# Sliding windows by DMA alone: 12 staged batches in place of 11, and nearly every direct DMA cut into 32 KB rows

## The chip, the cores and the metric

One core of one Trainium2 chip. The metric is the device time of one execution in microseconds. Executions of one kernel on one chip mostly agree within 0.3%. Every comparison of times below is made within one call (one session of runs), in which all kernels ran on the same chip beside runs of the kernel before. Each chip was used in one call only: what belongs to the chip and what to the call can't be told apart.

## The reference

The input `x` is 32 batches of 4096 rows of 256 floats. The output holds, for every batch, 127 windows of 64 rows, which start every 32 rows. Nothing is computed.

```python
n_windows = (length - window_size) // stride + 1      # 127
for i in range(n_windows):
    start = i * stride                                # stride 32
    result[:, i] = x[:, start:start + window_size]    # window_size 64
```

Think of a batch as 128 blocks of 32 KB (32 rows of 1 KB). Window `w` is block `w` followed by block `w + 1`, so nearly every block is written twice. The input is 134 MB, the output 266 MB.

## The kernel before

A batch goes one of two ways.

*Direct*: DMAs from DRAM to DRAM, issued from the sync queue. Every window is read and written: 8 MB through the DMA engines, 8 MB read and 8 MB written in HBM (the memory beside the chip, here the same as DRAM).

*Staged*: the 128 blocks are loaded once into a tile of 128 partitions (4 MB) and stored twice (8 MB), issued from the activation queue. The DMA engines carry 12 MB, HBM reads 4 and writes 8. A staged batch is therefore lighter on HBM and heavier on the DMA engines.

```python
DIRECT, IN, OUT = 32768, 16384, 16384    # packet sizes in bytes

def windows(self, q, b, w0, n, half=None):            # a direct DMA of n windows
    size = 2 * blk if half is None else blk           # half: only the first or second block of each
    off = blk if half else 0
    # out: n rows of `size` at window w0 of batch b; in: n rows, one block apart
    ...

class Staging:
    def run(self, q):                                 # groups of 6 batches: 6 loads, then 12 stores
        for first in range(0, len(self.batches), bufs):
            ...
            for g in group: self.load(q, g)
            for g in group: self.store(q, g)          # two stores of 128 rows of 32 KB each

# in the kernel:
staged = [*range(1, B - 3, 3), B - 2]                 # 11 batches; 21 are direct
for i, b in enumerate(direct):
    for j in range(7):                                # 7 times 16 windows, and later a "rest" of 15
        loading = turns < 102 or 306 <= turns < 391
        share += 5 if loading else 1
        cut = share >= 6
        turns += 4 if cut else 3
        if cut:                                       # two DMAs of 16 rows of 32 KB
            share -= 6
            c.windows(ring_d, b, w0 + 16 * j, 16, 0)
            c.windows(ring_d, b, w0 + 16 * j, 16, 1)
        else:                                         # one DMA of 16 rows of 64 KB
            c.windows(ring_d, b, w0 + 16 * j, 16)
    ...
```

The stores of a staged batch write 128 rows where 127 are wanted and so spoil one half window in each neighbouring batch. The "rest" DMA of the neighbour (15 windows) repairs it and waits for those stores. The last staged batch is stored exactly, in pieces of 112, 15, 15 and 112 rows.

`turns` is a count kept while the program is built. A DMA engine takes packets alternately from the two queues. A whole direct DMA gives each engine two 32 KB packets and one semaphore packet of 4 bytes (3 turns). A pair of cut ones gives two and two (4 turns). In as many turns the staged queue moves as many 16 KB packets. Cutting thus raises the staged share of the traffic.

## Time and profile before

| | before |
|---|---|
| time, median of the first 3 runs | 746.64 us (745.91 to 747.06) |
| time of the profiled run | 753.78 us (span 752.0) |
| direct 32 KB packets | 5334; shortest usual 1213 ns, mean 1239 |
| staged 16 KB packets | 8444; shortest usual 611 ns, mean 628 |
| semaphore packets | 4105; 9 ns |

The last three lines are from the packet records of the trace. "Shortest usual" is the value that more than half of the packets take; it is called the floor below.

These are lines of the page of the kernel before: the span, the busy share of the 16 DMA engines in 40 slices (tenths) and what they moved, the two queues (q1 direct, q10 staged; packets, MB, share of 16 engines' span) and the HBM traffic.

```profile
span 752.0 us, 308 instructions
...
DMA  9999999999999999999999999999999999999997
GB/s 372 422 419 432 424 435 427 414 426 416 416 425 422 423 424 416 422 421 420 421 421 395 424 423 424 431 429 417 429 416 414 416 422 425 417 429 420 417 393 302
DMA packets 17885, 313.16 MB, mean 416 GB/s; under 512 B 4105, under 2 KB 4105, under 8 KB 4105
...
q1 hardware_dynamic: 8881, 174.80, 55.2%
q10 hardware_dynamic: 9002, 138.35, 44.1%
...
HBM read 220.92 MB, written 266.99 MB: 649 GB/s over the span
```

The engines are busy up to the last slices, and the shares of the two queues add up to 99.3%. So an engine serves its packets one after another with hardly a gap, and the time is close to the sum of packet times on the engine that has the most. (The trace doesn't name the engine of a packet. How many packets an engine has is counted from the kernel; what is measured is the mean of all 16.)

The table of stretches of the same kernel (from and to in us, length, work of a compute engine, clock, DMA share, GB/s) shows the loads of a group of six (20 to 120, 420 to 510) and its stores (150 to 380, 535 to 660):

```profile
core 0: us, POOL busy (x), PEclk, DMA share, GB/s
20.00:120.00 100.00, 0.00 (x0) 1.00 1.00 424
150.00:380.00 230.00, 0.00 (x0) 1.00 1.01 422
420.00:510.00 90.00, 0.00 (x0) 1.00 1.00 425
535.00:660.00 125.00, 0.00 (x0) 1.00 1.01 419
```

The engines are full throughout, but in the store stretches they move 419 to 422 GB/s in place of 424 to 425. The packet records say why: direct packets take 1251 ns there, and 26% take more than 1270; in the load stretches they take 1219, and 2.5% do.

The DMA queues from 150 to 300 us (packets, MB, share), kernel before:

```profile
q1 hardware_dynamic: 1747, 36.18, 57.8%
q10 hardware_dynamic: 1745, 27.00, 42.7%
```

As many packets from one queue as from the other: this is the alternation by turns.

Two lines of the page's DMA issues (count, KB each, median us from issue to landing) show the mix of whole (1024 KB) and cut (512 KB) direct DMAs:

```profile
out_dram<-in_x_dram SPq DMA_DIRECT2D x92, 1024.0 KB, 100.3
...
out_dram<-in_x_dram SPq DMA_DIRECT2D x110, 512.0 KB, 91.0
```

### The profile page before, as it was taken

The page shows a single profiled execution, that of the slowest core. Times are in us where ns is not written, and L with a number is a line of the kernel's source. Part 1 is how long each engine was busy: PE and PEld are TensorE (multiplying, and loading weights), DVE is VectorE, ACT ScalarE, POOL GpSimd, SP SyncE. Part 2 cuts the span into 40 slices and gives each one's busy share as a digit, 9 for nine tenths or more (in the row PEclk, how much of TensorE's full clock was granted, in tenths as well). Part 3 has the DMA queues.
Part 4 walks back from the last instruction along what each step waited for, and adds up shares of the span by engine and source line. Part 5 has one row for each costly group of instructions (what it writes and reads, how often), then busy time and mean ns, then how long its engine had stood idle before and what let it go on. Part 6 is the DMA issues. An engine that isn't in the chain of part 4 may idle for free. (4 is left out here: it accounts for less than half of the span.)

```text
span 752.0 us, 308 instructions
## 1 busy us (share of the span) xinstructions
POOL 0.2 (0%) x4
## 2 busy tenths in 40 slices
POOL 0000000000000000000000000000000000000000
DMA  9999999999999999999999999999999999999997
GB/s 372 422 419 432 424 435 427 414 426 416 416 425 422 423 424 416 422 421 420 421 421 395 424 423 424 431 429 417 429 416 414 416 422 425 417 429 420 417 393 302
DMA packets 17885, 313.16 MB, mean 416 GB/s; under 512 B 4105, under 2 KB 4105, under 8 KB 4105
## 3 DMA queue, kind: packets, MB, share of 16 engines
q1 hardware_dynamic: 8881, 174.80, 55.2%
q10 hardware_dynamic: 9002, 138.35, 44.1%
q14 instruction: 2, 0.02, 0.0%
HBM read 220.92 MB, written 266.99 MB: 649 GB/s over the span
## 5 line engine op out<-in xcount | busy, mean ns | idle before, releaser
L187 POOL MEMSET const-bfloat16-1.0<- 128x1 bf16 x1 | 0.1, 103 | 0.0
L187 POOL MEMSET const-uint8-127<- 128x1 uint8 x1 | 0.1, 102 | 0.0
L187 POOL MEMSET const-float32-0.0<- 128x1 f32 x1 | 0.1, 100 | 0.2 <-issue 0.2
L187 POOL MEMSET const-float32-1.0<- 128x1 f32 x1 | 0.1, 99 | 0.0
## 6 DMA issues: line engine op xcount, KB each, us to landing
out_dram<-in_x_dram SPq DMA_DIRECT2D x92, 1024.0 KB, 100.3
out_dram<-xb ACTq DMA_DIRECT2D x20, 4096.0 KB, 142.4
out_dram<-in_x_dram SPq DMA_DIRECT2D x110, 512.0 KB, 91.0
xb<-in_x_dram ACTq DMA_DIRECT2D x11, 4096.0 KB, 124.0
out_dram<-in_x_dram SPq DMA_DIRECT2D x21, 960.0 KB, 99.2
out_dram<-xb ACTq DMA_DIRECT2D x2, 3584.0 KB, 100.5
out_dram<-xb ACTq DMA_DIRECT2D x2, 480.0 KB, 102.1
```

Source lines behind the costliest of these rows:

```text
L187: nc = _bacc.Bacc("TRN2", target_bir_lowering=False, num_devices=1)
```

## The change

The intent: give one more batch to staging, which takes traffic off HBM, and keep the two queues in balance by cutting nearly every direct DMA into 32 KB rows, in loads and in stores alike (12 of 12 and 11 of 12, in place of 5 of 6 and 1 of 6). The rests are issued when the count of turns says that the stores they wait for are done, with a slack of 34 turns.

```diff
-    staged = [*range(1, B - 3, 3), B - 2]
+    staged = [*range(1, B - 3, 3), B - 2, 0]
...
+    def rest_parts(b):
+        if len(waits[b]) == 2:            # batch 29 lies between two staged batches
+            return [(0, 8), (120, 7)]
+        return [(0 if b - 1 in spilled else 112, 15)]
...
-                loading = turns < 102 or 306 <= turns < 391
-                share += 5 if loading else 1
-                cut = share >= 6
-                turns += 4 if cut else 3
-                if cut:
-                    share -= 6
+                at = turns % (loads + per * stores)
+                share += 12 if at < loads else 11
+                if share >= 12:
+                    share -= 12
+                    turns += 4
...
+            rests.append(b)
+            rest(34)                      # rests whose stores are due, by the count of turns
```

More of the change, by code (lines that the diff above doesn't have):

```diff
@@ L33, in count, with windows @@
         self.total += 16
-    def windows(self, q, b, w0, n, half=None):
+    def windows(self, q, b, w0, n, half=None, piece=DIRECT, count=None):
         blk = self.blk
@@ L39, in windows @@
         off = blk if half else 0
-        self.count(
+        (count or self.count)(
             q.dma_start(
@@ L47, in windows @@
                 ),
-                max_dma_last_dim=DIRECT,
+                max_dma_last_dim=piece,
             )
@@ L132, with first @@
     spilled = staged[:-1]
-    def rest(b):
-        for n in (b - 1, b + 1):
-            if n in spilled:
-                st.wait_stored(ring_d, spilled.index(n))
-        c.windows(ring_d, b, 0 if b - 1 in spilled else 112, 15)
+    waits = {b: [g for g, n in enumerate(spilled) if abs(n - b) == 1] for b in direct}
+    per, loads, stores = 6, 6 * 17, 34
+    def first(b):
+        return 0 if b - 1 not in spilled else 8 if len(waits[b]) == 2 else 15
+    def rest_parts(b):
+        if len(waits[b]) == 2:
+            return [(0, 8), (120, 7)]
+        return [(0 if b - 1 in spilled else 112, 15)]
@@ L141, with stored_turn @@
+    def stored_turn(b):
+        return max(
+            [(g // per) * (loads + per * stores) + loads + (g % per + 1) * stores for g in waits[b]],
+            default=0,
+        )
     with tc.tile_critical():
         st.run(ring_s)
-        free = [b for b in direct if b - 1 not in spilled and b + 1 not in spilled]
-        direct = free + [b for b in direct if b not in free]
-        late = 8
-        share = turns = 0
-        for i, b in enumerate(direct):
-            w0 = 15 if b - 1 in spilled else 0
-            for j in range(7):
-                loading = turns < 102 or 306 <= turns < 391
-                share += 5 if loading else 1
-                cut = share >= 6
-                turns += 4 if cut else 3
-                if cut:
-                    share -= 6
-                    c.windows(ring_d, b, w0 + 16 * j, 16, 0)
-                    c.windows(ring_d, b, w0 + 16 * j, 16, 1)
-                else:
-                    c.windows(ring_d, b, w0 + 16 * j, 16)
-            turns += 3 if b in free or i >= len(free) + late else 0
-            if b in free:
-                rest(b)
-            elif i >= len(free) + late:
-                rest(direct[i - late])
@@ L168, with rest @@
-        for b in direct[-late:]:
-            rest(b)
+        turns = share = 0
+        rests = []
+        def rest(slack):
+            nonlocal turns
+            for b in list(rests):
+                if turns >= stored_turn(b) + slack:
+                    rests.remove(b)
+                    for g in waits[b]:
+                        st.wait_stored(ring_d, g)
+                    for w, n in rest_parts(b):
+                        c.windows(ring_d, b, w, n)
+                        turns += 3
@@ new lines @@
+        for b in direct:
+            for j in range(7):
+                at = turns % (loads + per * stores)
[3 more added lines that the diff above has]
+                    turns += 4
+                    c.windows(ring_d, b, first(b) + 16 * j, 16, 0)
+                    c.windows(ring_d, b, first(b) + 16 * j, 16, 1)
+                else:
+                    turns += 3
+                    c.windows(ring_d, b, first(b) + 16 * j, 16)
+            rests.append(b)
+            rest(34)
@@ L170 @@
+        rest(-10000)
         ring_d.wait_ge(c.done, c.total)
```

## The prediction

> **What bounds the kernel now.** The 16 DMA engines, which are full. The page's slices show DMA 9 up to the second last; the stretches table a DMA share of 1.00 with 419 to 425 GB/s from 20 to 675 us. The queue lines give 55.2% (direct) and 44.1% (staged) of 16 engines' span: packets are served one after another without gaps. By the trace's packet records a direct 32 KB packet takes 1213 ns at its floor, mean 1239; a staged 16 KB packet (load or store) 611, mean 628; a 4-byte semaphore packet 9. An engine moves 27 GB/s whatever the kind, so a staged batch (4 MB in, 8 MB out) costs it more than a direct one (8 MB). Its only gain is less HBM traffic (now 649 GB/s).
>
> That gain shows in the excess over the floors. In load stretches (20-135, 430-525 us), where most direct DMAs are already cut into 32 KB rows, direct packets take 1220 ns and 3% exceed 1270. In store stretches (160-395, 545-675 us), where one in six is cut, they take 1250 to 1255, and 26 to 28% exceed 1270: the mix is somewhat over what HBM serves.
>
> **The change.** The Trainium skill, "DMA: Bandwidth & Descriptors", section "Queues, rings and completion order", says that an engine alternates between queue rows packet by packet. The trace agrees: 1747 and 1745 packets from 150 to 300 us. A semaphore packet takes a turn, so cutting lets the staged queue move more bytes per direct byte. Turns per engine: 559 direct, 561 staged before; 615 and 612 after: balanced.
>
> - Removed per engine (0 to 6): 14 direct packets of 336, -17.0 us. The average engine loses 15.9: batch 29's rest becomes 8 + 7 windows, and by the same page's section "Why a DMA increments its semaphore by 16 and not by 1" a DMA of 15 rows uses 15 engines (3547 semaphore packets = 202x16 + 21x15 confirm it), so 8 and 7 rows load engines 0 to 6 twice.
> - Added: 48 staged packets, +29.3 us; about 73 semaphore packets, +0.7.
> - Floor of the fullest engine: 732.5 -> 745.5 us, +13.0.
> - Recovered: the stores' excess. I estimate direct packets at 1221 ns (as in load stretches), loads 625, stores 618: 393 + 120 + 237 + 3 = 753 us, against 416 + 332 + 2 = 750 now.
>
> All of it is on the critical path. Waits for stored tiles (64 us in two on the direct queue's issuer) cost nothing now, since issues run about 100 us ahead; the slack of 34 turns (estimate 45 us) should keep the queue full.
>
> So better HBM service and added bytes nearly cancel: +3 us on 746.6; zero excess would give -5. **Predicted 749 us, 743 to 757; faster by over 2%: 0.02; within: 0.94; slower: 0.04.**
>
> **What would show it.** Right: 317.4 MB in place of 313.2; HBM read about 216.8 MB; direct packets at 1215-1225 ns in store stretches, few over 1270; 424 to 430 GB/s there; both queues end together. Wrong: direct packets at 1240 or more in stores (then +10 us); a hole in the direct queue at a rest's wait; one queue outlasting the other.
>
> **What would make it wrong.** Excess set by HBM writes, not total traffic; more DMAs (293 for 223) making the issuer late; engines 0 to 6 ending over 2 us after the others.

The stretches named in it were read on the packet records' own clock, which runs 11 us ahead of the page's. The numbers of this document are read on the page's clock; they differ from those by less than 5 ns.

## The result, and the profile after

Ratios in this document are the mean time of one kernel's fast runs over that of the other's of the same rounds, so not quite the ratio of the medians that stand beside them.

| | before | after |
|---|---|---|
| time, median | 746.5 us (745.91 to 747.06, 4 runs) | 754.42 us (753.03 to 755.05, 4 runs) |
| ratio | | 1.0104 (95%: 1.0086 to 1.0121) |
| direct 32 KB packets, mean | 5334 at 1239 ns | 5080 at 1217 ns |
| staged 16 KB packets, mean | 8444 at 628 ns | 9212 at 617 ns |
| all packet times, per engine (mean of 16) | 747.1 us | 744.6 us |

The packets of before are those of its profiled run of 753.78 us, not of a run of 746.5. Profiles of both kernels on one chip stand under "Both kernels again".

The same lines of the page, kernel after:

```profile
span 752.5 us, 382 instructions
...
DMA  9999999999999999999999999999999999999995
GB/s 376 432 432 432 432 431 420 432 432 431 432 432 430 442 422 431 443 429 423 415 429 423 432 438 424 431 435 431 432 427 431 431 429 437 427 430 417 412 388 218
DMA packets 19552, 317.43 MB, mean 422 GB/s; under 512 B 5258, under 2 KB 5258, under 8 KB 5258
...
q1 hardware_dynamic: 9732, 166.48, 51.7%
q10 hardware_dynamic: 9818, 150.93, 47.3%
...
HBM read 216.79 MB, written 267.06 MB: 643 GB/s over the span
```

There are 4.3 MB more for the engines and 4.1 MB less to read from HBM, as intended. The rate of most slices rises to 430 GB/s and over. The last slice falls to 218 in place of 302: the engines are busy for 5 tenths of it in place of 7.

The same stretches, kernel after:

```profile
20.00:120.00 100.00, 0.00 (x0) 1.00 1.01 431
150.00:380.00 230.00, 0.00 (x0) 1.00 1.00 429
420.00:510.00 90.00, 0.00 (x0) 1.00 1.00 429
535.00:660.00 125.00, 0.00 (x0) 1.00 1.01 432
```

Stores now run as fast as loads, 429 to 432 GB/s. In the store stretches the direct packets take 1217 ns (1.3% over 1270) and the staged ones 612: the excess is all but gone. Sixteen engines at the floor of 32768 bytes in 1213 ns would move 432 GB/s, so this kernel stands at the limit of its engines.

The queues from 150 to 300 us, kernel after: they still alternate, but with more bytes on the staged side.

```profile
q1 hardware_dynamic: 1985, 33.59, 52.2%
q10 hardware_dynamic: 1998, 30.90, 48.1%
```

The same two kinds on the page of the kernel after:

```profile
out_dram<-in_x_dram SPq DMA_DIRECT2D x265, 512.0 KB
...
out_dram<-in_x_dram SPq DMA_DIRECT2D x8, 1024.0 KB
```

So the profile after shows nearly every packet faster than the profile before, and yet the kernel is 1% slower. The experiments are about this.

### The profile page after: what moved, and what is told of

Its sections match the earlier page's. It is cut to its first block, busy times and chain, and to the rows that moved or that the text cites. A ratio compares the mean times of both kernels' runs of the same rounds, so it can differ in the third digit from the quotient of the medians.

```text
span 752.5 us, 382 instructions
## 1 busy us (share of the span) xinstructions
POOL 0.2 (0%) x4
## 2 busy tenths in 40 slices
DMA packets 19552, 317.43 MB, mean 422 GB/s; under 512 B 5258, under 2 KB 5258, under 8 KB 5258
## 3 DMA queue, kind: packets, MB, share of 16 engines
q1 hardware_dynamic: 9732, 166.48, 51.7%
q10 hardware_dynamic: 9818, 150.93, 47.3%
HBM read 216.79 MB, written 267.06 MB: 643 GB/s over the span
```

## The experiments

Three calls were made. All twelve runs finished; the result of one is wrong, on purpose. The chips of the three calls are called B, A and C, by what they did with the kernel before: B and C took 753.5 and 753.9 us for it, A took 747.1.

| run | chip | time, us | ratio to before (95%) | direct, staged packet, ns |
|---|---|---|---|---|
| before again | B | 752.96 | 0.9985 (0.9965 to 1.0005) | 1237, 627 |
| before, third | C | 753.77 | 0.9997 (0.9984 to 1.0009) | 1238, 627 |
| after again | B | 756.76 | 1.0038 (1.0020 to 1.0056) | 1220, 619 |
| after, third | A | 754.23 | 1.0109 (1.0085 to 1.0133) | 1216, 617 |
| after, fourth | C | 757.33 | 1.0042 (1.0029 to 1.0055) | 1219, 619 |
| 11 staged, all cut | B | 758.70 | 1.0065 (1.0046 to 1.0084) | 1254, 619 |
| 12 staged, old cuts | B | 774.91 | 1.0272 (1.0243 to 1.0300) | 1239, 640 |
| 12 staged, whole rows, same mix | A | 754.11 | 1.0098 (1.0081 to 1.0114) | 1218, 617 |
| 11 staged, even cuts | A | 745.37 | 0.9984 (0.9966 to 1.0002) | 1225, 623 |
| 11 staged, even cuts, again | C | 753.97 | 0.9995 (0.9983 to 1.0007) | 1235, 631 |
| 12 staged, batch 29's rest spread | A | 751.12 | 1.0061 (1.0044 to 1.0078) | 1216, 617 |
| 12 staged, last store whole (wrong result) | C | 756.20 | 1.0031 (1.0018 to 1.0044) | 1220, 617 |

The theory: the time is the sum of packet times on the fullest engine. The change adds 13.0 us to that sum at the floor and takes away the excess over the floor, which stems from more HBM traffic than HBM serves. How much excess there is to take away depends on the chip. The rivals: the form of the rows (64 or 32 KB) and not the mix of traffic sets the excess; the many small DMAs cost the 8 us; the end of the kernel does.

### Both kernels again, on three chips

No edit. The kernel before:

> The kernel before, unchanged, profiled again. Theory A: the profiled execution of before (753.8 us) was a poor sample of its timed runs (746.5), so its excess over the floors was overstated: a run near 746 should show direct packets at about 1228 ns and staged ones at about 621, sum of packet times about 740 us per engine in place of 747. Rival: the profiler itself costs this kernel 7 us every time: again about 753 us when profiled, direct 1239, staged 628. Ratio 1.000 in either case.

> The kernel before, unchanged, for a profile on whichever chip this call gets. Theory (its excess depends on the chip): if this call's times are near 747, direct packets at about 1227 ns and staged about 622, sum of packet times about 741 us per engine; if near 753, 1237 and 627, as in the earlier look, sum 746. Rival (the difference between chips lies outside the packets, in start or end): 1237 and 627 in either case.

The kernel after:

> The changed kernel, unchanged. Both theories: about 754 us, ratio 1.010; direct packets 1217 ns, staged 617, sum of packet times 745 us per engine.

> The changed kernel again, as the reference for the other runs of this call. Before moved between two chips (746.5 and 753.5 us) and the changed kernel less (754.4 and 756.8). Theory: before runs at the edge of what HBM serves and so shows the chip's state, the changed kernel runs at the engines' floor and does not: 754 to 757 us, ratio 1.003 to 1.011, high where before is near 746. Rival: the chips differ alike for both kernels: a ratio that stays at the same value whatever before shows.

> The changed kernel as reference of this call: 754 to 757 us; direct 1216 to 1220 ns, staged 617 to 619; ratio to before about 1.010 where before is near 747, about 1.004 where it is near 753.

The first run did not decide: the time itself was 753 us on this chip, timed and profiled runs alike, so neither expectation applied as it stood. What it did show is that the profiler doesn't cost 7 us. (On A it doesn't either: the kernel with even cuts took 745.71 us profiled and 745.03 to 746.61 otherwise.) So the first profile of before was most likely taken on another chip than its timed runs; the record doesn't say which chip it was. The third look at before fell on a chip of 753.8 us and could not decide either, because both theories expected about 1237 and 627 ns there. So no profile of before at 747 us exists.

The kernel after answers the larger question. Its ratio is 1.0109 on A, where before takes 747 us, and 1.0038 and 1.0042 on B and C, where before takes 753.5 to 753.9. The rival, the same ratio everywhere, falls. From chip to chip before moved by 7 us and after by 3.

B also gives what the first two profiles could not, both kernels profiled on one chip. From 150 to 380 us, before and then after:

```profile
150.00:380.00 230.00, 0.00 (x0) 1.00 1.01 422
```

```profile
150.00:380.00 230.00, 0.00 (x0) 1.00 1.01 428
```

In the store stretches direct packets go from 1247 to 1222 ns and staged ones from 626 to 614 (on C from 1250 to 1222 and from 626 to 614). So the excess shrinks on one and the same chip, and the time still rises, by 3.2 us on B.

That most of the difference between chips lies in the packets is shown by another kernel with 11 staged batches, the one with even cuts (below), which was profiled on both sorts of chip: its packet times sum to 739.6 us per engine on A and 746.9 on C, 7.3 us apart, where the profiled runs are 9.6 us apart. For the kernel after they sum to 744.2 on A and 746.4 on C. The kernel with more HBM traffic depended more on the chip; these are two kernels only.

### The cut alone: 11 staged batches, every direct DMA cut

```diff
-                share += 5 if loading else 1
+                share += 6
```

> The kernel before with 11 staged batches, every direct DMA cut into 32 KB rows: the cut alone, 651 direct turns per engine against 561 staged. Theory (the mix of traffic sets the excess): packets at the floor while both queues run (direct 1217 ns, staged 615), then some 42 direct packets per engine alone at the end, at about 1213 x 864/661 = 1585 ns: +15 us there, in all about 752 us (748 to 758), HBM-bound tail of about 65 us with the staged queue empty. Rival (the row form alone sets the excess, or only bytes count): direct packets stay at 1217 to the end, about 738 us.

It took 758.70 us, ratio 1.0065, just above the expected band, and the mechanism is as expected. The stretches of this kernel:

```profile
150.00:380.00 230.00, 0.00 (x0) 1.00 1.01 430
535.00:660.00 125.00, 0.00 (x0) 1.00 1.01 428
690.00:735.00 45.00, 0.00 (x0) 1.00 0.93 325
```

Up to 660 us the stores run at 428 to 430 GB/s: cutting alone removes the excess (direct packets 1217 ns in store stretches). At 678 us the staged queue has nothing left. The direct queue is then alone; its line for 690 to 735 us:

```profile
q1 hardware_dynamic: 830, 14.62, 93.5%
```

Direct packets take 1501 ns here, with a share of busy engines of 0.93 (some 15 of the 16), and 325 GB/s are moved, which is 650 GB/s of reads and writes in HBM. It is the same kind of packet as before, at 1.24 times the floor. Bytes alone or the form of the rows don't explain this. Nor is it that a queue without a second one beside it is slow. The same trace settles that: later about 12 engines have work, still with direct packets alone.

```profile
746.00:750.00 4.00, 0.00 (x0) 1.00 0.76 328
```

From 746 us on all 61 direct packets take the floor of 1213 ns, and 12 engines move as much as 15 did. So the limit is one that the engines share, on what they read and write in DRAM together. That it lies in HBM and not on the way to it is the natural reading, but not shown. The limit isn't one sharp number, though. By the queue lines shown above, the store stretches of before put 421 x (1 + 36.18 / 63.18) = 662 GB/s on HBM, with excess, and those of after 430 x (1 + 33.59 / 64.49) = 654, nearly without; direct copies alone, which read as much as they write, are held to 650. At the floor of all 16 engines the three mixes would ask for 432 x 1.573 = 679, 432 x 1.521 = 657 and 432 x 2 = 864: the more is asked for above some 655, the longer the packets. One reason that the prediction feared, an excess set by HBM writes alone, falls by the same numbers: in store stretches every byte moved is written, and this rate rose from 421 to 430 GB/s while the excess went.

### The staging alone: 12 staged batches, cut as before

```diff
-                share += 12 if at < loads else 11
+                share += 10 if at < loads else 2
```

> The changed kernel with 12 staged batches, cut as before (5 of 6 in loads, 1 of 6 in stores): 539 direct turns against 612 staged. Theory (added bytes on the fullest engine cost +13 us, cutting gives back the stores' excess): excess returns in stores (direct 1235 to 1250 ns, staged 622 to 628), about 760 us (756 to 765), the last 45 us staged packets alone at their floor. Rival (the many small DMAs and semaphores cost the 8 us): about 748 us.

It took 774.91 us, far from the rival's 748 and 10 us over the upper end of the theory's band. The excess in the stores came back as expected: 1249 ns for direct packets, 624 for staged ones. So fewer small DMAs (217 in place of 293) don't make it faster. As the end of this run is bad in its own right, that alone doesn't clear them; their semaphore packets do, at 9 ns each 3.0 us per engine in the kernel after and 2.3 in before. What had been underestimated is the end. Its stretches:

```profile
150.00:380.00 230.00, 0.00 (x0) 1.00 1.01 421
535.00:660.00 125.00, 0.00 (x0) 1.00 1.01 422
735.00:760.00 25.00, 0.00 (x0) 1.00 0.92 264
760.00:774.00 14.00, 0.00 (x0) 1.00 0.35 147
```

The direct queue runs out of work at about 700 us, because its 539 turns are fewer than the 612 of the staged queue (by the program's count), and its last rests have to wait for stores that come at turn 578. From 735 us the engines move 264 GB/s and then 147. Two things happen there: work that comes too late for the engines, and slow stores of the last batch (see the last experiment). The packet records part them in size. The profiled run is 20.1 us longer than that of after on this chip, and the packet times account for 17.5 of these (764.1 us per engine against 746.6). Staged packets alone exceed their floor by 7.3 us per engine after 735 us, and take 961 ns up to 760. So slow packets, in the stores and above all at the end, are the larger part, idle engines the smaller; why the packets are that slow was not tested here. A kernel with two queues needs them to end together; here it took 15 us more than the 760 that the mix and the bytes had led to expect.

### The mix without the cut

Every direct DMA is whole, and after each two of them comes a tiny DMA (16 rows of 32 bytes into a scratch tile). It uses the two turns which the two cuts had used. The mix of bytes per turn is the same, the rows are 64 KB, and there are 161 direct DMAs, rests among them, and 66 tiny ones.

```diff
-                if share >= 12:
-                    share -= 12
-                    turns += 4
-                    c.windows(ring_d, b, first(b) + 16 * j, 16, 0)
-                    c.windows(ring_d, b, first(b) + 16 * j, 16, 1)
-                else:
-                    turns += 3
-                    c.windows(ring_d, b, first(b) + 16 * j, 16)
+                turns += 3
+                c.windows(ring_d, b, first(b) + 16 * j, 16)
+                if share >= 24:
+                    share -= 24
+                    turns += 2
+                    c.tiny(ring_d, scratch, tinies)
+                    tinies += 1
```

> The changed kernel with every direct DMA whole (64 KB rows), and after each two of them one tiny DMA of 512 bytes whose data and semaphore packets take the two turns that the two cuts took: same mix per turn, no cut. Theory (the mix takes the excess away): direct packets 1217 to 1222 ns, staged 612 to 620, 754 to 759 us (some 70 tiny DMAs at an estimated 0.05 us each). Rival (the row form takes it away): in stores direct 1240 to 1255, staged 625 to 630, about 762 to 767 us.

The queues over the whole run carry the same as in the kernel after (9732 packets, 166.48 MB, and 9818, 150.93 MB):

```profile
q1 hardware_dynamic: 9732, 166.51, 51.7%
q10 hardware_dynamic: 9818, 150.93, 47.3%
```

754.11 us beside 754.23 for the kernel after on the same chip, and in the store stretches direct packets of 1218 ns and staged ones of 613, beside 1217 and 612 with cuts. The rival's 1240 ns came from a profile on another chip and may be too high a mark for A; what counts is that nothing changes. The size of the rows makes no difference that these runs show. Cutting works through the turns that its extra packets take. The 227 DMAs here in place of 293 make no difference either.

### The same cuts spread evenly, 11 staged batches

```diff
-                share += 5 if loading else 1
-                cut = share >= 6
+                share += 3
+                cut = share >= 8
 ...
-                    share -= 6
+                    share -= 8
```

> The kernel before with its 11 batches and the same number of cuts (3 of 8), spread evenly over loads and stores in place of 5 of 6 and 1 of 6. Theory (excess grows with the mix and is the same for reads and writes): packets alike in all stretches, direct about 1235 ns, staged about 620, time within 4 us of before. Rival (loads bear less than stores, so the uneven split is needed): load stretches with direct packets over 1250 and time 5 us or more above before.

> Eleven batches, cuts spread evenly, again. It was 0.9984 of before (0.9966 to 1.0002) on a chip where before was near 747. Theory (even mix lowers the excess of the stores, where HBM is the limit): 0.5 to 3 us less than before here too, more if this chip's before is near 753. Rival: it was noise, ratio 1.000 within 0.001.

This was an attempt at a version better than both. It isn't one that can be told from before: 0.9984 on A and, with five rounds, 0.9995 on C, both intervals with 1 inside. (An identical kernel scored 0.9985 on B, so that is the size of noise.) The expectation that it would gain more on a chip of 753 us was wrong. The first stretch of loads and of stores, on A and then on C:

```profile
20.00:120.00 100.00, 0.00 (x0) 1.00 1.00 423
150.00:380.00 230.00, 0.00 (x0) 1.00 1.00 429
```

```profile
20.00:120.00 100.00, 0.00 (x0) 1.00 1.00 415
150.00:380.00 230.00, 0.00 (x0) 1.00 1.01 424
```

At the same mix the loads now run slower than the stores, 423 against 429 and 415 against 424 GB/s, while the direct packets take about the same time in both (1226 and 1224 on A, 1233 and 1239 on C). The staged ones differ: 631 in load stretches against 615 in store stretches on A, 643 against 622 on C. So the part of the theory fell that the excess is the same for reads and writes: the loads bear less here, and the uneven split of before was about as good as the even one. Direct packets alone, which the rival had named, don't show it.

### Who ends last: the rest of batch 29

As the prediction counts, the two DMAs of 8 and 7 windows fall on the same engines, 0 to 6 (the trace doesn't name engines). In this version each is spread over all 16 engines, in pieces of 4 KB:

```diff
+    def spread(self, q, b, w0, n):
+        blk, s = self.blk, self.blk // 8
+        self.count(
+            q.dma_start(
+                out=self.oap((b * self.nw + w0) * 2 * blk, [[s, 16], [2 * blk, n], [1, s]]),
+                in_=self.xap(b * self.nb + w0, [[s, 16], [blk, n], [1, s]]),
+            )
+        )
...
-                        c.windows(ring_d, b, w, n)
+                        if n < 15:
+                            c.spread(ring_d, b, w, n)
+                        else:
+                            c.windows(ring_d, b, w, n)
```

> The changed kernel with batch 29's rest of 8 and 7 windows spread over all 16 engines in 4 KB pieces (two DMAs). Theory (engines 0 to 6 end last, because the rest falls on them twice): their 322 packets become 318 and 15 small ones of about 160 ns: 2.5 us less than the changed kernel, 752 to 754 us where that has 755 to 757. Rival (the end is set by the staged queue or by waits): no change within 1 us.

751.12 us beside 754.23 on the same chip, with intervals apart (1.0044 to 1.0078, 1.0085 to 1.0133). The gain of 3.1 us is somewhat more than the 2.5 expected, while the packets' mean times are the same (1216 and 617 ns): what is left as the cause is balance between the engines. The direct queue's last packet ends at 747.5 us in place of 750.4. This is better than the changed kernel, and still 0.6% slower than the kernel before on this chip.

### The slow packets of the last batch

In the profile after, staged packets take 665 ns from 690 to 735 us, and 5.7% of them over 1000. There the last staged batch is stored in pieces of 112 and 15 rows. In this version it is stored in two DMAs of 128 rows. The second one is shifted by one window to stay inside the output, so the result of that batch is wrong.

```diff
-            for half, p0, rows in ((0, 0, 112), (0, 112, 15), (1, 1, 15), (1, 16, 112)):
-                self.c.count(self.c.store(q, self.tiles[i], self.batches[g], half, p0, rows))
+            for half in (0, 1):
+                self.c.count(self.c.store(q, self.tiles[i], self.batches[g], half, shift=half))
```

> The changed kernel with the last staged batch stored in two DMAs of 128 rows in place of 112, 15, 15 and 112 rows (wrong second halves in that batch, on purpose). Theory (rows that are not split evenly over the engines make staged packets collide): staged packets after 680 us at 611 to 620 ns instead of 630 to 700, 2 to 3 us less than the changed kernel. Rival (it is the end of the kernel that slows them): still 630 to 700 ns there, no change within 1 us.

Staged packets from 690 to 735 us took 613 ns and none took over 1000; in the kernel after on the same chip, 660 ns and 4.8%. The end of the kernel as such doesn't slow them; the division into 112, 15, 15 and 112 rows does (how it does was not tested). The stretches of the kernel after on this chip, and then of this version:

```profile
700.00:720.00 20.00, 0.00 (x0) 1.00 0.96 399
720.00:740.00 20.00, 0.00 (x0) 1.00 0.94 388
```

```profile
700.00:720.00 20.00, 0.00 (x0) 1.00 0.96 410
720.00:740.00 20.00, 0.00 (x0) 1.00 0.94 401
```

The time fell by 1.1 us only (757.33 to 756.20), less than expected, and the intervals overlap (1.0029 to 1.0055, 1.0018 to 1.0044), so a gain in time isn't shown. One reason may be that the direct queue ends last in both (753.9 and 751.9 us), and the staged one, 4.8 and 6.1 us earlier; this was not tested further.

## Why the prediction was right or wrong

The prediction was 749 us with 743 to 757, and "within 2%" at 0.94. Measured: 754.42, within 2%. It was right, but its centre was 5 us low, and by errors of opposite sign that partly cancelled: before had been taken 7 us too low, and the packets of after some 3 us too slow.

- **What bounds the kernel: right.** Both kernels keep the DMA engines full, and every packet has the same floor as before (1213, 611 and 9 ns).
- **What is added: right.** 317.43 MB (317.4 predicted) and 216.79 MB read (216.8), 293 direct DMAs. The floor of the fullest engine goes from 732.5 to 745.5 us.
- **What is recovered: the mechanism right, shown by the runs with the cut alone and with the mix alone.** (Shown is that the mix sets the excess; that it is HBM which limits is argued.) Direct packets in store stretches take 1217 ns (1215 to 1225 predicted) at 429 to 432 GB/s (424 to 430). The estimate for after, 753 us for the fullest engine, was a little too cautious for the chip of its first profile: 322 direct packets at 1217 ns, 576 staged at 617 and 3 us of semaphores make 750 us, with the loads at 612 ns in place of the 625 that had been assumed. On B the packets of both kernels give 749 us before and 752 after by the same sum: there the sums of the prediction, 750 and 753, hold.
- **The fullest engine: right.** The prediction had the uneven rest in its sum (322 direct packets on engines 0 to 6, where engines 8 to 14 have 318 by the kernel's count) and feared that these engines end over 2 us after the others. How much later each ended the trace doesn't tell; spreading the rest gave 3.1 us. Of the 7.2 us between the medians on A (747.05 and 754.23), these are 3.1; the other 4.1 are the added bytes less the recovered excess.
- **The step that failed in size: "against 416 + 332 + 2 = 750 now".** That sum is taken from packets of a run of 753.78 us, and the difference of 3 us was then put on 746.6 us, the time of other runs. Packets at 1239 and 628 ns don't belong to a run of 746.6 us: as the floors are the same in every profile, the profiled run must have had some 7 us more excess than the timed ones (not seen, as no profile of before at 747 us exists). That much recovery was counted which the timed runs didn't have to give. Where before did run like its profile, on chips B and C, the ratio was 1.0038 and 1.0042, and the predicted +3 us on 747 would be 1.004. Where it ran at 747 us, on A, the ratio was 1.0109. The 753 us that the same sum gave for after would have come nearer, but by luck: a run takes some 4 us more than that sum (753.78 against 750), and the sum was 3 us too high.
- **The queues: partly right.** "Both queues end together" held for before (750.2 us each) and not quite after: the staged queue ended at 746.1 us, the direct one at 750.9. The waits of the direct queue's issuer for stores at its rests (126 us in ten, and 41 us in one more) made no visible hole.

What stays open: no profile of before at 747 us was caught, so its packets on such a chip are known only through the kernel with even cuts, which has the same bytes (739.6 us per engine on A). What differs between the chips, or between the calls, was not looked into. And why the staged packets are so slow at the end of the run with the old cuts isn't known.

## What to carry to other kernels

When two resources are both near their limits, moving load from one to the other can yield less than one sum alone says: here 13 us of engine time were paid for an excess that was worth 18 us at most (750 less the floor of 732.5), and less where before took 747 us. Before you subtract something measured in a profile from a median, check that the profiled run took the median time. Where engines alternate between queues packet by packet, as these do, small packets are a knob for the mix of traffic, and the queues should end together, on every engine.

## What the Trainium skill lacked or had wrong

- "DMA: Bandwidth & Descriptors", section "Specifications", gives about 27 GiB/s per engine. The floor here is 32768 bytes in 1213 ns, 27.0 GB/s, which is 25.2 GiB/s; sixteen of these make 432 GB/s, which does agree with the page's fabric ceiling of 435 GB/s.
- "HBM Reference", section "Specifications (TRN2)", gives about 716 GB/s per domain, without saying how reads and writes count. With direct DRAM to DRAM copies alone, one core got 325 GB/s moved, or 650 GB/s read and written together, with the other queue empty, and as much with 12 engines busy as with 15.
- "DMA: Bandwidth & Descriptors", section "Queues, rings and completion order", tells of the alternation by packets, and calls some 9 to 17 descriptors typical of one. In these traces single records of 32 KB, 16 KB or 4 bytes come in equal numbers from both queues (1747 and 1745 from 150 to 300 us). So the page lacks that a 4-byte semaphore packet (9 ns) takes a whole turn against a 16 KB one (611 ns), and that the number of DMAs thereby sets the shares of two queues. The run with tiny DMAs shows it: same packet times and same time (754.11 and 754.23 us) without any cut.
- No page states that stores from a tile in 112 and 15 rows run slower per packet than those of 128: 660 against 613 ns in the same stretch. The section "Why a DMA increments its semaphore by 16 and not by 1" of the same page tells how many engines such a DMA uses (15 rows: 15 engines, confirmed by 3547 semaphore packets), but nothing of collisions. "SBUF — State Buffer", section "SBUF: two separate sides", does name the ports between SBUF and the DMA engines as a place where several engines can contend, without a number for such stores. Whether this is the cause wasn't tested.
- No page states that such a kernel differs from chip to chip (or call to call): before took 747.1, 753.5 and 753.9 us on three of them, and after 754.2, 756.8 and 757.3.
